# Gate of the output norm in a hybrid decoder layer: a weighted sum on VectorE in place of matrix products with a broadcast column

## The chip, the cores and the metric

One core of one Trainium2 chip runs the whole kernel as one program. The metric is the time of one execution on the device, in microseconds; the lower the better. Engines are called by their names and, in the profile, by short ones: TensorE (PE, and PEld for its loads of weights), VectorE (DVE), ScalarE (ACT), GpSimd (POOL) and SyncE (SP), whose queue issues nearly all transfers.

## The reference, cut to what matters

The layer normalises its input, scales and shifts it by vectors that depend on a condition c, runs three token mixers and multiplies the normed output by a third vector, the gate. All three vectors come from one product of silu(c), 1024 long, with a matrix of 1024x3072:

```python
mod = jnp.einsum('bd,de->be', jax.nn.silu(c), w_ada) + b_ada
shift, scale, gate = jnp.split(mod[:, None, :], 3, axis=-1)
h = rms_norm(x, g_pre) * (1.0 + scale) + shift
proj = jnp.einsum('bsd,de->bse', h, w_in)
...
return x + gate * rms_norm(out, g_post)
```

Everything is in fp32; x is 1024 tokens by 1024 channels. The gate is used at the very end only, shift and scale at the start: no column of h exists before its part of them.

## The kernel before, in words

The program is written with a scheduler: the code lists operations with their tiles, and a list scheduler sets the order on each engine when the program is built. Each engine then runs its list strictly in order. A change in one place can so reorder others.

The start (lines 241 to 441) works on eight depth tiles kt of 128 channels. x is normed (norm_x) and transposed into xT[kt], channels on partitions. `modulate(kt)` (line 355) multiplies and adds the tile's scale and shift and splits the result into two parts hh and hl, hi and lo, for three products in place of one exact one: ScalarE copies hh (line 110), VectorE subtracts for hl (line 112). The same split is made of weights (wh, wl). `first_products(kt)` (line 414) then adds the tile's 16 matmuls of 512 columns to three pairs of sums: ps_gq (queries of the gated linear attention, GLA), ps_gk (keys) and ps_n (small projections). The loop over kt at line 423 also calls `modulation(j)` for the next pair of tiles, issues the loads that are due, and calls `gate(0)` and `gate(1)` at kt = 5 and 7.

`modulation` and `gate` both stand on `gemv(j)` (line 324). A set of w_ada, four tiles of 4x256 columns, 512 KB each, is multiplied by the column sc = silu(c), broadcast to 32 columns as weights: four depth tiles run side by side in the four column groups of the array, so that pr holds four partial sums, each 32 times over (16 products, which the profile shows as 32 instructions). ScalarE copies pr to ar (line 333), four transposes pt put the 512 sums on partitions (line 337), and a reduction on VectorE adds the four groups into mc (line 339). `modulation` makes shift and scale of it (lines 345 to 347), `gate` makes half of the gate, 512 channels (lines 352 and 353). A transpose pgt (line 438) and ScalarE's copy grow turn the gate into rows, which SyncE stores to gate_d; it is read back for the output stage at line 1278.

The tiles of w_ada live in nine rotating buffers (line 258), six sets of four through nine slots: a load waits until the product that used its slot is done. SyncE issues in order; on its queue between the loads stand the weights wr_gv and wr_gq of the next projections. wr_gq has the buffer that wr_gv had, so it is issued when VectorE has split that (wl_gv).

Behind the loop come the projection of the GLA values (ps_gv, line 167 to 169), the gates of GLA (psl, line 537, from lrf, which is made of ps_n) and the chunked scan, whose products (psc, pk, pd, pso) the scheduler threads between those of the projections. The change touches only `load_gate`, `load_wa` and `gate`.

Of the kernel before, what the change touches and what calls it, by code (L numbers as in the profile page):

```python
# [8 lines left out]
F32 = mybir.dt.float32  # L9
# [3 lines left out]
ALU = mybir.AluOpType  # L13
# [3 lines left out]
P = 128  # L17
S = 1024
D = 1024
HALF = 512  # L20
NK = D // P
# [8 lines left out]
def kernel(  # L30
# [21 lines left out]
    nc = tc.nc  # L52
    V, A, G, T = nc.vector, nc.scalar, nc.gpsimd, nc.tensor
# [9 lines left out]
    def open_pool(name, **kw):  # L63
        stack = ExitStack()
        return stack.enter_context(pool(name, **kw)), stack
# [16 lines left out]
    def bank(tag, name, shape=(P, HALF)):  # L82
        if tag == "acc":
            return ps_acc.tile(list(shape), F32, tag="acc", name=name, bufs=2)
        return ps_acc.tile(list(shape), F32, tag=tag, name=name, bufs=BANKS[tag])
# [19 lines left out]
    def const(shape, name, dt=F32):  # L105
        return cst.tile(shape, dt, tag=name, name=name)
# [76 lines left out]
    XT = ["x0", "x1", "x2", "x3", "x4", "x5"]  # L183
    GT = ["g0", "g1", "g2", "g3"]

    def sh(tag, name, shape=(P, S), dt=F32):
        return shr.tile(list(shape), dt, tag=tag, name=name, bufs=3 if tag == "t" else 1)
# [14 lines left out]
    one_col = const([P, 1], "one_col")  # L202
# [5 lines left out]
    sc = const([P, NK], "sc")  # L208
# [6 lines left out]
    for li, b in enumerate(LV):  # L215
        m = gmask[:, li, :].rearrange("p (n b) -> p n b", b=b)
        n = 64 // b
# [18 lines left out]
    st_pool, st_stack = open_pool("start", side="right")  # L236
# [13 lines left out]
    wa = []  # L250
    ring = [0]

    def load_wa(cols):

        parts = {}
        for z in range(2):
            for kh in range(2):
                t = sh((GT + ["t"] * 3 + XT[0:2])[ring[0] % 9], f"wa{len(wa)}{z}{kh}", (P, 4, 256))
                ring[0] += 1
                nc.sync.dma_start(t, w_ada[0, kh * 512 : (kh + 1) * 512, cols[z] : cols[z] + 256].rearrange(  # L260
                    "(k p) e -> p k e", p=P))
                parts[z, kh] = t
        wa.append(parts)

    def load_mod(j):

        load_wa((j * 256, D + j * 256))

    def load_gate(u):
        load_wa((2 * D + u * 512, 2 * D + u * 512 + 256))  # L270

    xn = [st_pool.tile([P, D], F32, tag=f"xn{st}", name=f"xn{st}") for st in range(8)]

# [50 lines left out]
    def gemv(j):  # L324

        pr = bank("b", f"pr{j}", (P, 2, 256))
        for z in range(2):
            for kh in range(2):
                for k in range(4):
                    T.matmul(pr[32 * k : 32 * k + 32, z, :], sc[:, 4 * kh + k : 4 * kh + k + 1].to_broadcast([P, 32]),  # L330
                             wa[j][z, kh][:, k, :], start=(kh == 0), stop=(kh == 1))
        ar = st_pool.tile([P, 4, P], F32, tag="ar", name=f"ar{j}", bufs=2)
        A.copy(ar, pr.rearrange("p z (c e) -> p (z c) e", e=P))

        pt = bank("d", f"pt{j}", (P, 4, P))
        for i in range(4):
            T.transpose(pt[:, i, :], ar[:, i, :], ident)
        mc = st_pool.tile([P, 4], F32, tag="mc", name=f"mc{j}", bufs=2)
        V.tensor_reduce(mc, pt.rearrange("p a (g r) -> p a g r", r=32)[:, :, :, 0], axis=AX.X, op=ALU.add)
        return mc  # L340
# [6 lines left out]
        V.tensor_tensor(out=modc[:, 1, js], in0=pt[:, 2:4], in1=gpre[:, js], op=ALU.mult)  # L347

    def gate(u):
        pt = gemv(4 + u)  # L350
        us = slice(4 * u, 4 * u + 4)
        V.tensor_tensor(out=modc[:, 2, us], in0=pt, in1=bgt[:, us], op=ALU.add)
        V.tensor_tensor(out=modc[:, 2, us], in0=modc[:, 2, us], in1=gpost[:, us], op=ALU.mult)
# [69 lines left out]
    for kt in range(NK):  # L423
        if kt in (0, 2, 4):
            modulation(kt // 2 + 1)
        if kt == 0:
            load_mod(3)
        elif kt in (2, 4):
            load_gate(kt // 2 - 1)
        if kt in (5, 7):  # L430
            gate((kt - 5) // 2)
        if kt + 1 < NK:
            modulate(kt + 1)
        first_products(kt)
# [21 lines left out]
    for i, hs in halves():  # L456
# [6 lines left out]
                               op0=ALU.add, op1=ALU.add)  # L463
# [82 lines left out]
    for i in range(3):  # L546
        t = gp.tile([P, 4, 2, 64], F32, tag=f"qbd{i}", name=f"qbd{i}")
# [3 lines left out]
    for i in range(2):  # L551
        t = gp.tile([P, 4, P], F32, tag=f"scs{i}", name=f"scs{i}")
# [347 lines left out]
    def pair(col, name, f, fin, fn=None):  # L900

        o, done = {}, {}

        def dst(j):
            o[j] = big(f"o{j}_{name}") if f is plain else small_out(j, name)
            return o[j]

        def post(j, i, hs):
            if fn is not None:
                with tc.high_priority():  # L910
                    fn(o[j][:, hs], f"{name}{j}{i}")
            done[j] = done.get(j, 0) + 1
            if done[j] == 2:
                fin(j, o[j])

        f(col, name, dst, post)
        return o
# [80 lines left out]
    for q in range(2):  # L998
        u = pair(C_PU + q * 256, f"pu{q}", seven, lambda j, t: None)
# [283 lines left out]
    for st in range(8):  # L1283
# [6 lines left out]
        for ci, (c0, c1) in enumerate(zip(cuts, cuts[1:])):  # L1290
            n, w = c0 // HALF, c1 - c0
# [54 lines left out]
```

## Time and profile before

| what | value |
|---|---|
| median of 3 runs | 1110.08 us (1108.61 to 1112.13) |
| profiled execution | 1112.2 us, its span 1110.5 us |
| TensorE busy | 1062.0 us, 96% of the span |
| VectorE, ScalarE, GpSimd busy | 67%, 42%, 34% |
| mean granted clock of TensorE | 0.99 |

The span is what the profiler saw of one execution, from the first instruction to the last; 1.7 us of that execution's time lie around it. Matmuls are pipelined: a matmul of 512 columns is shown with 0.39 us, but the next one starts 0.23 us after it, so costs on TensorE are read from start to start. In the timeline a number in brackets is the engine's idle time before the row and what ended it.

### The profile page before, as it was taken

How to read it: one execution, taken by the hardware profiler on the slowest of the kernel's cores; microseconds unless marked ns; L12 is line 12 of the kernel's file. 1: busy time of each engine (PE TensorE's matmuls, PEld its weight loads, DVE VectorE, ACT ScalarE, POOL GpSimd, SP SyncE). 2: the span in 40 equal slices, each digit the busy share in tenths (PEclk: the TensorE clock that was granted, in tenths of full speed). 3: DMA queues.
4: the chain of work that ended last, by engine and by line, in shares of the span. 5: the costliest groups of instructions: out<-in, count | busy, mean ns of one | idle time of the engine just before them, and what ended most of it. 6: DMA issues, size and time to landing. Idle time of an engine off the chain costs nothing.

```text
span 1110.5 us, 15436 instructions
## 1 busy us (share of the span) xinstructions
PE 1062.0 (96%) x5599; PEld 858.0 (77%) x5599; DVE 745.5 (67%) x1403; ACT 461.8 (42%) x877; POOL 382.8 (34%) x339
## 2 busy tenths in 40 slices
PE   5899999999998999899999999999998999999997
PEld 3579888987887888688878888886676776787886
DVE  6637689576898768997665756547574769487323
ACT  6336446344634332443433444336443437343111
POOL 1023153033374345445554545421200434343000
PEclk9999999999999999999999999999989899999999
DMA  9930111301333433256754333369949552463232
GB/s 317 305 109 20 39 35 44 101 25 48 117 114 97 152 115 114 72 195 218 254 171 133 98 131 114 114 189 359 259 154 297 187 167 86 171 216 135 83 107 76
DMA packets 97776, 159.33 MB, mean 143 GB/s; under 512 B 8266, under 2 KB 71324, under 8 KB 97700
## 3 DMA queue, kind: packets, MB, share of 16 engines
q1 hardware_dynamic: 97348, 157.54, 44.6%
q8 instruction: 44, 0.72, 0.3%
q10 hardware_dynamic: 352, 0.80, 0.2%
q14 instruction: 32, 0.26, 0.1%
HBM read 113.16 MB, written 45.16 MB: 143 GB/s over the span
## 4 chain that ended last, share of the span: by engine, by line
PE 68%; DVE 13%; DMA 10%; issue 3%; POOL 2%; ACT 2%; SPq 1%; DVEq 0%; ACTq 0%; POOLq 0%
PE pp_m L146 6%; PE pp_m L144 6%; PE pp_m L145 6%; PE po L1156 3%; PE psy L144 3%; PE psy L146 3%; PE psy L145 3%; PE pso L1298 3%; PE pso L1297 3%; PE pso L1296 3%; PE psc L655 2%; PE tp L1146 2%; DMA wa<-in_w_ada_dram 2%; DMA m_in<-m_d 1%; DVE win L969 1%
## 5 line engine op out<-in xcount | busy, mean ns | idle before, releaser
L144 PE MATMUL psy<-ogh,wh_y 128*128 128x512 f32 x192 | 77.6, 410 | 7.5 <-DMA ogh<-ogh_d 3.6
L146 PE MATMUL psy<-ogh,wl_y 128*128 128x512 f32 x192 | 75.6, 402 | 1.9 <-DVE wl_y L114 1.7
L145 PE MATMUL psy<-ogl,wh_y 128*128 128x512 f32 x192 | 77.1, 401 | 0.0
L144 PE MATMUL pp_m<-hh,w_m 128*128 128x512 f32 x192 | 74.8, 390 | 0.6 <-ACT w_m L110 0.6
L146 PE MATMUL pp_m<-hh,w_m 128*128 128x512 f32 x192 | 74.8, 390 | 0.5 <-DVE w_m L112 0.5
L145 PE MATMUL pp_m<-hl,w_m 128*128 128x512 f32 x192 | 74.7, 389 | 0.0
L112 DVE TENSOR_TENSOR w_m<-wr_m,w_m 128x512 fp32r<-128x512 f32 x36 | 43.1, 1202 | 39.8 <-ACT w_m L110 39.8
L1052 POOL TENSOR_SCALAR_AFFINE_SELECT Fd<-F 128x128 f32<-128x128 f32 x64 | 22.2, 350 | 132.5 <-DVE mx L1074 90.2
L1081 ACT ACTIVATE t<-t,ng 128x1024 f32<-128x1024 f32 (+3 forms) x64 | 49.6, 776 | 39.4 <-DVE ng L1079 36.6
L112 DVE TENSOR_TENSOR w_m<-S_m,w_m 128x512 fp32r<-128x512 f32 x48 | 56.6, 1206 | 3.7 <-ACT w_m L110 2.9
L1069 DVE CUSTOM_DVE_ANT_0 t<-psL,F 128x512 f32<-128x512 f32 (+2 forms) x80 | 41.2, 524 | 22.4 <-PE psL L1066 10.7
L566 POOL TENSOR_TENSOR e<-cum 128x256 f32<-128x256 f32 x24 | 18.6, 777 | 101.0 <-DVE ko L598 23.7
L793 POOL TENSOR_TENSOR sb<-hh,hl 128x512 f32<-128x512 f32 x16 | 22.0, 1408 | 86.7 <-PE pr L330 66.4
L957 ACT ACTIVATE o_m<-o_m 128x512 f32<-128x512 f32 x48 | 29.1, 629 | 54.9 <-DVE o_m L858 34.6
L1297 PE MATMUL pso<-wol,mh 128*128 128x512 f32 (+1 forms) x136 | 51.2, 377 | 0.0
L1296 PE MATMUL pso<-woh,mh 128*128 128x512 f32 (+1 forms) x136 | 51.2, 376 | 0.0
L1298 PE MATMUL pso<-woh,ml 128*128 128x512 f32 (+1 forms) x136 | 51.0, 376 | 0.0
L144 PEld LDWEIGHTS psy<-ogh,wh_y 128*128 128x128 f32 x192 | 37.2, 194 | 16.2 <-DMA ogh<-ogh_d 3.9
L1300 DVE TENSOR_TENSOR yo<-pso,gb 128x512 f32<-128x512 f32 (+1 forms) x17 | 11.2, 661 | 55.8 <-ACT jk L1299 55.8
L1148 ACT COPY PT<-tp 128x512 f32<-128x512 f32 (+1 forms) x64 | 31.6, 504 | 39.5 <-PE tp L1146 36.1
L1146 PE MATMUL tp<-ident,t 128*128 128x128 f32 x288 | 45.4, 280 | 2.0 <-ACT t L1081 1.1
L1156 PE MATMUL po<-PT,vf 128*64 128x256 f32 (+1 forms) x320 | 45.6, 366 | 0.0
(585 smaller groups left out, 3332.9 us busy)
## 6 DMA issues: line engine op xcount, KB each, us to landing
wa<-in_w_ada_dram SPq DMA_DIRECT2D x24, 512.0 KB, 8.8
wr_m<-in_w_in_dram SPq DMA_DIRECT2D x24, 512.0 KB, 3.7
m_d<-o_m SPq DMA_DIRECT2D x24, 512.0 KB, 2.9
m_in<-m_d SPq DMA_DIRECT2D x24, 512.0 KB, 6.7
xn<-in_x_dram SPq DMA_DIRECT2D x8, 512.0 KB, 6.2
kl<-fkl_d SPq DMA_DIRECT2D x16, 256.0 KB, 8.9
kk<-fkh_d SPq DMA_DIRECT2D x16, 256.0 KB, 10.6
F<-fc_d SPq DMA_DIRECT2D x8, 512.0 KB
```

What stands on the lines that cost most here:

```text
L112: j = (E or V).tensor_tensor(out=lo, in0=raw, in1=hi.bitcast(F32), op=ALU.subtract)
L144: T.matmul(ps, wh, rh, start=first, stop=False)
L145: T.matmul(ps, wh, rl, start=False, stop=False)
L146: T.matmul(ps, wl, rh, start=False, stop=last)
L1069: V.tensor_tensor_reduce(out=t[:, c0:e], in0=ps[:, : e - c0], in1=Fb[p, h][:, c0:e], scale=1.0, scalar=-3e38, op0=ALU.subtract, op1=ALU.ma ...
L1081: A.activation(t[:, :W], t[:, :W], AF.Exp, bias=ng[:, 0:1], accum_out=sm)
L1146: T.transpose(tp[:, j, :], t[:, kb * P : (kb + 1) * P], ident)
L1148: A.copy(pts[h, kg][:, 0:nb, qs], tp[:, 0:nb, :])
L1156: T.matmul(po[64 * h : 64 * h + 64, q0:256], vf[p // 2, kb // 4][:, kb % 4, col : col + 64], pts[h, kb // 4][:, kb % 4, q0:256], start=(kb ...
L1296: T.matmul(ps[:, :w], mh[k][:, sl], hi, start=(k == 0), stop=False)
L1297: T.matmul(ps[:, :w], mh[k][:, sl], lo, start=False, stop=False)
L1298: T.matmul(ps[:, :w], ml[k][:, sl], hi, start=False, stop=(k == NK - 1))
```

## The change

The gate no longer uses `gemv`. Its set of w_ada is loaded as four tiles of two depth tiles by 512 columns: 512 KB each as before, in contiguous pieces of 2 KB in place of 1 KB. VectorE multiplies the first depth tile by its column of sc and adds the other seven, weighted, onto it: gacc, 128x512, one weighting and seven weight-and-adds. The sum over the 128 partitions is made by four products in which gacc is the weights (128 columns at a time) and a column of ones moves: ptg, 128x4, in place of sixteen products, a copy, four transposes and a reduction. The two operations of the gate that follow read ptg from PSUM.

```diff
+    def wa_tile(name, shape):
+        ring[0] += 1
+        return sh((GT + ["t"] * 3 + XT[0:2])[(ring[0] - 1) % 9], name, shape)
...
     def load_gate(u):
-        load_wa((2 * D + u * 512, 2 * D + u * 512 + 256))
+        parts = []
+        for n in range(4):
+            t = wa_tile(f"wg{u}{n}", (P, 2, HALF))
+            c0 = 2 * D + u * HALF
+            nc.sync.dma_start(t, w_ada[0, n * 256 : (n + 1) * 256, c0 : c0 + HALF].rearrange("(k p) e -> p k e", p=P))
+            parts.append(t)
+        wa.append(parts)
...
     def gate(u):
-        pt = gemv(4 + u)
+
+        acc = st_pool.tile([P, HALF], F32, tag="gacc", name=f"gacc{u}", bufs=2)
+        V.tensor_scalar(out=acc, in0=wa[4 + u][0][:, 0, :], scalar1=sc[:, 0:1], scalar2=None, op0=ALU.mult)
+        for k in range(1, NK):
+            V.scalar_tensor_tensor(out=acc, in0=wa[4 + u][k // 2][:, k % 2, :], scalar=sc[:, k : k + 1], in1=acc,
+                                   op0=ALU.mult, op1=ALU.add)
+        pt = bank("d", f"ptg{u}", (P, 4))
+        for i in range(4):
+            T.matmul(pt[:, i : i + 1], acc[:, i * P : (i + 1) * P], one_col, start=True, stop=True)
         us = slice(4 * u, 4 * u + 4)
         V.tensor_tensor(out=modc[:, 2, us], in0=pt, in1=bgt[:, us], op=ALU.add)
```

The new lines move the code behind them by 9 lines (from modulation's transposes on) to 17. The scheduler's order moves with the change at two places that the prediction speaks of.

VectorE around `modulation(3)`, which makes shift and scale of the depth tiles 6 and 7. mc3 is the sum that it starts from, modc the tile of shifts, scales and gate, xT6, ht0 and ht1 the modulated tiles, and wl_gq1 the lo part of the next projection's weights, whose hi part wh_gq1 ScalarE makes when the load wr_gq1 has landed. Before:

```order
L339 TENSOR_REDUCE mc3_673<-pt3_668 128x4
L345 TENSOR_TENSOR modc_190<-mc3_673,colv_186 128x2
L346 TENSOR_TENSOR mc3_673<-mc3_673,colv_186 128x2
L347 TENSOR_TENSOR modc_190<-mc3_673,colv_186 128x2
L363 TENSOR_SCALAR xT6_256<-xT6_256,modc_190 128x512 x2
L363 TENSOR_SCALAR ht0_764<-xT7_257,modc_190 128x512
L363 TENSOR_SCALAR ht1_768<-xT7_257,modc_190 128x512
L112 TENSOR_TENSOR wl_gq1_1326<-wr_gq1_1323,wh_gq1_1325 128x1024
```

And with the change, from the first of the three small operations on (gacc0 and gacc1 are the sums of the two halves of the gate, wg12 and wg13 its last two loads):

```order
L354 TENSOR_TENSOR modc_190<-mc3_673,colv_186 128x2
L355 TENSOR_TENSOR mc3_673<-mc3_673,colv_186 128x2
L112 TENSOR_TENSOR wl_gq1_1302<-wr_gq1_1299,wh_gq1_1301 128x1024
L363 SCALAR_TENSOR_TENSOR gacc1_776<-wg12_682,sc_189,gacc1_776 128x512
L356 TENSOR_TENSOR modc_190<-mc3_673,colv_186 128x2
L369 TENSOR_TENSOR modc_190<-ptg0_719,colv_186 128x4
L363 SCALAR_TENSOR_TENSOR gacc1_776<-wg13_684,sc_189,gacc1_776 128x512
L380 TENSOR_SCALAR xT6_256<-xT6_256,modc_190 128x512 x2
L370 TENSOR_TENSOR modc_190<-modc_190,colv_186 128x4
L380 TENSOR_SCALAR ht0_752<-xT7_257,modc_190 128x512
```

The split wl_gq1 stood behind the modulated tiles and stands ahead of them now, in the middle of the small operations, with operations of the gate behind it.

TensorE around the first products of depth tile 6, those that read hh6. Before (pr4, the products of the first half of the gate, stand ten rows ahead of this piece):

```order
L421 MATMUL ps_n1_473<-hl5_687,wnr_408 128x512
L144 MATMUL ps_gq00_470<-hh6_738,wh_gq0_244 128x512
L144 MATMUL ps_gk00_474<-hh6_738,wh_gk0_248 128x512
L420 MATMUL ps_n0_472<-hh6_738,wnr_408 128x512
L144 MATMUL ps_gq01_471<-hh6_738,wh_gq0_244 128x512
L144 MATMUL ps_gk01_475<-hh6_738,wh_gk0_248 128x512
L420 MATMUL ps_n1_473<-hh6_738,wnr_408 128x512
L337 MATMUL pt4_729<-ident_177,ar4_727 128x128 x4
L330 MATMUL pr5_788<-wa500_678,sc_189 32x256 x4
L330 MATMUL pr5_788<-wa501_680,sc_189 32x256 x4
```

With the change:

```order
L438 MATMUL ps_n1_473<-hl5_687,wnr_408 128x512
L367 MATMUL ptg0_719<-one_col_184,gacc0_710 128x1 x4
L144 MATMUL ps_gq00_470<-hh6_726,wh_gq0_244 128x512
L144 MATMUL ps_gk00_474<-hh6_726,wh_gk0_248 128x512
L437 MATMUL ps_n0_472<-hh6_726,wnr_408 128x512
L144 MATMUL ps_gq01_471<-hh6_726,wh_gq0_244 128x512
L144 MATMUL ps_gk01_475<-hh6_726,wh_gk0_248 128x512
L437 MATMUL ps_n1_473<-hh6_726,wnr_408 128x512
L367 MATMUL ptg1_785<-one_col_184,gacc1_776 128x1 x4
```

The products and transposes of the gate are gone; the column products of the first half stand between tiles 5 and 6, those of the second half behind the first six products of tile 6.

## Rows read from the trace of the kernel before

**Rows 1.** Windows: length, busy us of PE, PEld, DVE, ACT, POOL; clock, DMA, GB/s

```profile
76.00:300.00 224.00, 222.45 (x1510) 191.32 (x1509) 163.63 (x264) 110.89 (x216) 68.14 (x77) 1.00 0.17 51
```

**Rows 2.** Timeline of PE, 60 to 76 us: start, length, engine, line, operation

```profile
60.62 1.93 PE L330 MATMUL pr<-wa,sc 128*32 128x256 f32 x32
62.49 0.50 PE L144 MATMUL ps_gk<-hh,wh_gk 128*128 128x512 f32 x1
...
64.99 0.50 PE L144 MATMUL ps_gq<-hh,wh_gq 128*128 128x512 f32 x1
...
66.50 0.60 PE L337 MATMUL pt<-ident,ar 128*128 128x128 f32 x4
...
68.03 0.50 PE L145 MATMUL ps_gq<-hl,wh_gq 128*128 128x512 f32 x1
...
70.52 1.07 PE L330 MATMUL pr<-wa,sc 128*32 128x256 f32 x16
71.52 0.50 PE L144 MATMUL ps_gq<-hh,wh_gq 128*128 128x512 f32 x1
...
75.31 0.60 PE L337 MATMUL pt<-ident,ar 128*128 128x128 f32 x4
75.66 0.36 PE L167 MATMUL ps_gv<-wh_gv,hh 128*128 128x256 f32 x1
```

**Rows 3.** Timeline of ACT; in brackets the idle time before, and its releaser

```profile
63.35 1.06 ACT L110 ACTIVATE wh_gq<-wr_gq 128x1024 fp32r<-128x1024 f32 x1 [7.66 <-DMA wr_gq<-in_w_in_dram]
64.32 1.14 ACT L110 ACTIVATE hh<-xT 128x512 fp32r<-128x512 f32 x2
```

**Rows 4.** Timeline of DVE, 54 to 67 us

```profile
54.78 1.29 DVE L112 TENSOR_TENSOR hl<-xT,hh 128x512 fp32r<-128x512 f32 x2
...
61.21 0.16 DVE L347 TENSOR_TENSOR modc<-mc,colv 128x2 f32<-128x2 f32 x1
61.41 1.00 DVE L363 TENSOR_SCALAR xT<-xT,modc 128x512 f32<-128x512 f32 x2
...
64.44 1.23 DVE L112 TENSOR_TENSOR wl_gq<-wr_gq,wh_gq 128x1024 fp32r<-128x1024 f32 x1 [1.12 <-ACT wh_gq L110]
```

**Rows 5.** Timeline of PE around a product with one column (pf)

```profile
191.47 0.28 PE L167 MATMUL ps_gv<-wh_gv,hh 128*128 128x256 f32 x1
191.59 0.28 PE L509 MATMUL pf<-fx,seg 128*128 128x1 f32 x2
...
191.93 0.28 PE L169 MATMUL ps_gv<-wh_gv,hl 128*128 128x256 f32 x1
```

**Rows 6.** DVE: weight-and-adds, in the timeline and in groups by line

```profile
89.92 1.22 DVE L476 SCALAR_TENSOR_TENSOR gl0l<-lx,gl0l 128x1024 f32<-128x1024 f32 x1 [0.79 <-ACT gl0l L473]
...
L114 DVE SCALAR_TENSOR_TENSOR wl_y<-wr_y,wh_y 128x512 fp32r<-128x512 f32 x24 | 23.1, 964 | 0.0
```

**Rows 7.** Windows as in rows 1: loads in pieces of 1 KB, then 4 KB

```profile
50.00:54.00 4.00, 4.00 (x22) 3.04 (x22) 0.36 (x1) 1.45 (x2) 0.00 (x0) 1.00 1.09 348
...
856.00:860.00 4.00, 0.89 (x6) 0.41 (x4) 1.55 (x7) 2.09 (x6) 0.29 (x1) 0.98 1.03 410
```

**Rows 8.** Timeline of PE: a product that waited for its load; the first of tile 4

```profile
47.27 0.63 PE L330 MATMUL pr<-wa,sc 128*32 128x256 f32 x6 [0.86 <-DMA wa<-in_w_ada_dram]
...
54.95 0.50 PE L144 MATMUL ps_gq<-hh,wh_gq 128*128 128x512 f32 x1
```

**Rows 9.** Timeline of PE: restarts after two stops, and where the pace returns

```profile
353.73 0.50 PE L144 MATMUL pp_zp<-T4h,w_zp 128*128 128x512 f32 x1 [3.51 <-DVE o_zp L990]
...
358.17 0.39 PE L144 MATMUL pspl<-dh,wph 128*128 128x512 f32 x1
...
806.01 0.79 PE L144 MATMUL psy<-ogh,wh_y 128*128 128x512 f32 x1 [3.19 <-DVE mrg L1214]
...
812.12 0.39 PE L145 MATMUL psy<-ogl,wh_y 128*128 128x512 f32 x1
```

**Rows 10.** Windows as in rows 1: a stretch at the low clock

```profile
862.00:866.00 4.00, 4.00 (x12) 3.12 (x11) 1.21 (x4) 0.37 (x1) 0.00 (x0) 0.50 1.03 410
```

More of the change, by code (lines that the diff above doesn't have):

```diff
@@ L257, in load_wa @@
             for kh in range(2):
-                t = sh((GT + ["t"] * 3 + XT[0:2])[ring[0] % 9], f"wa{len(wa)}{z}{kh}", (P, 4, 256))
-                ring[0] += 1
+                t = wa_tile(f"wa{len(wa)}{z}{kh}", (P, 4, 256))
                 nc.sync.dma_start(t, w_ada[0, kh * 512 : (kh + 1) * 512, cols[z] : cols[z] + 256].rearrange(
```

## The prediction, made before the changed kernel was run

> **What bounds the kernel now.** I read three views in this order. First the windows: from 76 to 300 us TensorE is busy for 222.45 of 224 us [rows 1], so there a microsecond that TensorE is late by is a microsecond on the end, and one that it is early by is won. Then the timeline of TensorE over the stretch in which the gate is made. It runs without a pause from the gate's products (pr at 60.62) to the first product of the next stage (ps_gv at 75.66) [rows 2]. I use 75.66 as the mark: the time at which that product starts says what the change is worth. Last the timelines of ScalarE and VectorE beside it. They tell what TensorE would be waiting for at 64.99: the products of depth tile 6 need hh6, whose two halves start on ScalarE at 64.32, behind wh_gq, which had waited 7.66 us for a transfer and started at 63.35 [rows 3]. VectorE had the tile xT6 ready long before, from 61.41 [rows 4]. So before the change the gate's first set of products, 60.62 to 62.49, fills time in which TensorE would otherwise have waited for hh6. Taking it away wins nothing by itself.
>
> **The change, part by part.**
>
> *TensorE, removed.* The first gate's products: 62.49 - 60.62 = 1.87 us. Its transposes with half of the second's products: 68.03 - 66.50 = 1.53. The other half: 71.52 - 70.52 = 1.00. The last transposes: 75.66 - 75.31 = 0.35 [rows 2]. Together 4.75 us.
>
> *TensorE, added.* Eight products with one column. The trace has one of these forms, pf: the ps_gv products around it would follow each other by 0.12 us, so that the third would come at 191.71, and it comes at 191.93 [rows 5]; 0.22 us each, 0.9 us for a gate's four, 1.8 us for both. As work alone TensorE gains 4.75 - 1.8 = 3.0 us.
>
> *VectorE, added.* Two weightings of 128x512 (nearest row: xT, two in 1.00 us, so 0.5 each [rows 4]) and fourteen weight-and-adds. That form, with all operands in SBUF, takes 1.22 us for 1024 columns, so 0.61 for 512; the slowest group of its size shows 0.96 [rows 6]. I take 0.61, the nearest row in time and in kind. In all 9.5 us, in a stretch where VectorE has gaps. The two removed reductions are 0.17 each and ScalarE's two copies of pr lie in gaps: nothing.
>
> *Where they stand.* The order shows what matters. Before, the four small operations of modulation 3, xT6 and ht come first and the split wl_gq after them. Now wl_gq stands inside modulation 3, with a weight-and-add, the last small operation, the first addition for the gate and another weight-and-add between it and xT6. wl_gq cannot start before wh_gq is done, and that waits for the transfer of wr_gq. So the tile that TensorE needs next is queued behind a transfer.
>
> *When wr_gq lands.* Its place in SyncE's queue is unchanged, its issue waits for wl_gv, and what now stands ahead of that on VectorE needs a load that lands before wl_gv's own; the queue is never empty meanwhile. In the trace it is there at 63.35 [rows 3]. Seven of the gate's eight loads of 512 KB are ahead of it. In pieces of 1 KB such loads come at 348 GB/s, 1.51 us each; loads in pieces of 4 KB came at 410 [rows 7]. The gate's pieces grow from 1 to 2 KB. The bounds are no gain and the gain of 4 KB, 1.51 - 1.28 = 0.23 us a load. From two rows, 47 ns for 1 KB and 160 ns for 4 KB on each of 16 engines, 2 KB is 84 ns by a straight line, 390 GB/s, 1.34 us a load: an estimate. I take this: 7 x 0.16 = 1.1 us, wr_gq at 62.25. The Trainium skill (DMA: Bandwidth & Descriptors, Specifications) has full line rate from pieces of 512 B on. By that rule 2 KB is no faster than 1 KB and wr_gq lands at 63.35, which would put the sum below at 1113.4. The trace disagrees: pieces of 1 and of 4 KB are both longer than that, and came at 348 and at 410 GB/s.
>
> *VectorE to hh6.* TensorE got a load at 47.27 [rows 8]. The gate's first is the second behind it, there at 50.3. The first weighting waits for it ahead of hl4 on VectorE, so that hl4 is done at about 52.1; TensorE comes to tile 4 at 54.95 [rows 8]: nothing. The first load of the second half of the gate is the seventh behind, 47.27 + 7 x 1.51, less five gains: about 57.0. hl5 is done at 54.78 + 1.29 = 56.07 [rows 4]. From 57.0 a weighting, six weight-and-adds, the reduction, two more and two small operations (0.2 each, 61.41 - 61.21 [rows 4]) end at 57.0 + 0.5 + 8 x 0.61 + 0.6 = 63.0 (at 0.96 each, 2.8 later; that end belongs to the last rival). wh_gq is done at 62.25 + 1.06 = 63.3. Then wl_gq 1.23, 0.61, 0.2, 0.2, 0.61 and half of xT6 0.5: 66.65. ScalarE's half of hh6 takes some 0.6, and TensorE starts at about 67.3 (68.4 if the transfer is no faster).
>
> *TensorE's stop.* Without the first gate's products it is through with tile 5 at 64.99 - 1.87 = 63.1, the four column products end at 64.0, and it stops for 3.3 us (4.4). Before, it had no stop here. From hh6 to the mark there were 75.66 - 64.99 = 10.67 us; less 2.88 of gate work, plus 0.9 and the transpose pgt of 0.1 (moved ahead of the mark) it is 8.8. The mark comes at 76.1 (77.2): later by 0.5 (1.6).
>
> *The clock.* A stop as long as this is not free on this kernel. After one of 3.51 us, twelve matmuls of 512 columns fill the 4.44 us from 353.73 to 358.17, where at the usual 0.228 they need 2.74: 1.7 us lost. After one of 3.19 us, thirteen of them and two of 128 columns fill the 6.11 us from 806.01 to 812.12 in place of 3.08: 3.05 lost [rows 9]. The granted clock in such a stretch is 0.50, 1.2 GHz, the lower of the two levels, and it comes back some time after the restart [rows 10]. The second stretch is low from its restart on, the first only from its fifth matmul. The bounds are 0 and 3.05; I take 1.7, from the stop that is nearest in length.
>
> *The rest.* SyncE's queue now issues gate_d ahead of ff_d; both are read much later. The scan's operations stand 1 to 3 us later in TensorE's order, and so does what feeds them (psl waits for lrf, whose copies now end behind all products); TensorE has the projections to do meanwhile. Nothing from there.
>
> **Sum.** 0.5 + 1.7 = 2.2 us later. The profiled execution took 1112.2 us (span 1110.5), so 1114.4; the median of the runs is 2.1 us below it, and the forecast is **1112.3 us** beside 1110.08. About 0.3%, 3.3 us, is what can be told from no change, so this counts as the same.
>
> **The rivals.** *No stop.* If wr_gq lands some 3 us sooner than worked out and VectorE is through its adds by then, TensorE keeps its gain of 3.0 us: 1107.1. For it: the 3.0 us are work taken from an engine that is hardly idle after [rows 1]. Against: 63.35 is a measured arrival, and the order puts it ahead of xT6.
>
> *A stop, but no fall of the clock.* 0.5 us: 1110.6. For it: 3.3 us is hardly more than the 3.19 shown, and two stops are little evidence. Against: both of them were followed by the low pace.
>
> *The longer pieces gain nothing.* wr_gq lands at 63.35 as before, the stop is 4.4 us, everything behind it is 1.1 later: 1.6 + 1.7 = 3.3, 1113.4. For it: the only rows at the gate's own load are at 348 GB/s, none shows pieces of 2 KB under load. Against: the rate rises with the piece between the two rows that there are. The rule of the Trainium skill named above would lead here.
>
> *The stop outlasts the fall of the clock (slower).* Place: TensorE's wait for hh6. If TensorE restarts only after the clock has gone down, as at 806.01, the price is 3.05 instead of 1.7. It decides from the point at which hh6 comes later than the fall, and a stop of 4.4 us makes that likelier than one of 3.3. Between 0.5 + 3.05 = 3.55 and 1.6 + 3.05 = 4.65; the middle gives 1114.2. For it: of the two stops shown the shorter ended this way. Against: the other did not, and it is the nearer in length.
>
> **How the numbers follow.** Forecast 0.44, no stop 0.10, no fall 0.10, no gain from the pieces 0.14, long fall 0.22. Under 1106.8 lies near half of the no-stop case and a little else: faster 0.06. Over 1113.4 lie half of the case of the pieces, most of the long fall, and a little of the forecast, by what the reshuffled scan may add: 0.07 + 0.19 + 0.04, slower 0.30. The same: 0.64. The forecast's own range is 1110.5 to 1114; over the cases, 1108.3 at the low end leaves out the no-stop rival, and 1115.3 at the high end takes in 4.65 and half a microsecond of the scan.
>
> **What would show it.** On VectorE wl_gq before xT6, xT6 starting near 66 instead of 61.41; on TensorE a wait of 3 to 5 us for hh6 (the line of ps_gq, released by ScalarE) after the four column products; a granted clock under 1 in the windows just after; ps_gv starting at 77 to 79. The transfer of wr_gq at 62.3 or at 63.4 settles the pieces. I am wrong if TensorE shows no wait there, or if the end moves by another amount than the mark: then the scan was reshuffled for better or worse.

## The result, and the profile after

The changed kernel is **slower by 0.78%**: ratio 1.0078, interval [1.0056, 1.0099]. Its median is 1116.5 us (1114.49 to 1119.81, seven runs), that of the kernel before beside it 1109.86. The two medians alone lie 6.6 us apart; by the ratio, which is the measure used here, it is 8.7 us, interval 6.2 to 11. The forecast of 2.2 us later and the range's end of 1115.3 were too low. The profiled execution took 1115.91 us, its span 1114.2. The kernel before had medians of 1109.86, 1107.69 and 1107.02 us beside the three sets of runs told of here, so kernels are compared by their ratios to it. The work behind the change stands 17 lines lower now; the experiments move it by a few more.

TensorE after the change, in the timeline that answers to [rows 2]:

```profile
62.62 0.39 PE L438 MATMUL ps_n<-hl,wnr 128*128 128x512 f32 x1
63.68 1.02 PE L367 MATMUL ptg<-one_col,gacc 128*128 128x1 f32 x8 [0.67 <-DVE gacc L363]
69.05 0.80 PE L144 MATMUL ps_gq<-hh,wh_gq 128*128 128x512 f32 x1 [4.35 <-ACT hh L110]
```

Tile 5 ends with the product at 62.62. (The profile shows the four column products of a half as eight instructions.) The predicted wait is there, between the column products of the first half and the first product that reads hh6. It is 4.35 us long, and a wait of 0.67 us for VectorE's adds stands ahead of it. The mark, the first product of ps_gv, comes at 81.45 us instead of 75.66. VectorE, which answers to [rows 4]:

```profile
58.32 0.49 DVE L361 TENSOR_SCALAR gacc<-wg,sc 128x512 f32<-128x512 f32 x1 [0.43 <-DMA wg<-in_w_ada_dram]
58.73 4.06 DVE L363 SCALAR_TENSOR_TENSOR gacc<-wg,sc,gacc 128x512 f32<-128x512 f32 x6
62.70 0.17 DVE L348 TENSOR_REDUCE mc<-pt 128x4 f32<-128x16 f32 x1
...
64.25 1.22 DVE L112 TENSOR_TENSOR wl_gq<-wr_gq,wh_gq 128x1024 fp32r<-128x1024 f32 x1
...
66.85 2.90 DVE L380 TENSOR_SCALAR xT<-xT,modc 128x512 f32<-128x512 f32 x2
...
72.70 3.25 DVE L112 TENSOR_TENSOR hl<-ht,hh 128x512 fp32r<-128x512 f32 x2
```

From 58.73 to 76 us no row of VectorE has a bracket: it goes from one operation to the next without a pause, and xT6, at 61.41 before, starts at 66.85. Two things were not foreseen: wl_gq does not wait for its transfer, VectorE comes to it late; and the two halves of xT6 take 2.90 us where they took 1.00 [rows 4]. ScalarE and GpSimd beside it:

```profile
62.74 1.06 ACT L110 ACTIVATE wh_gq<-wr_gq 128x1024 fp32r<-128x1024 f32 x1 [7.02 <-DMA wr_gq<-in_w_in_dram]
68.37 0.63 ACT L110 ACTIVATE hh<-xT 128x512 fp32r<-128x512 f32 x1 [4.57 <-DVE xT L380]
```

```profile
66.36 3.11 POOL L810 TENSOR_TENSOR sb<-hh,hl 128x512 f32<-128x512 f32 x2 [61.44 <-DVE modc L369]
71.62 3.79 POOL L810 TENSOR_TENSOR sb<-hh,hl 128x512 f32<-128x512 f32 x2 [2.15 <-ACT hh L110]
```

GpSimd's sums of half tiles (sb, a helper of the later projections) lie beside the two operations that have become long, xT6 and hl7. Before, they waited for the second gate's products on TensorE:

```profile
71.27 5.04 POOL L793 TENSOR_TENSOR sb<-hh,hl 128x512 f32<-128x512 f32 x4 [66.36 <-PE pr L330]
```

In the row at 66.36 the bracket names the operation of VectorE that came last, its first addition for the gate. In the changed kernel and in two of those below (e6_half, e7_xt6_first) alike, though, GpSimd starts 0.22 to 0.23 us after the end of the second half's fifth weight-and-add, the last that reads the third load, so it is this add that the sums wait for. The windows (length, busy us of PE, PEld, DVE, ACT, POOL; clock, DMA, GB/s):

```profile
50.00:54.00 4.00, 4.00 (x19) 3.02 (x18) 2.35 (x4) 1.08 (x2) 0.00 (x0) 1.00 1.06 379
...
64.00:68.00 4.00, 0.70 (x7) 0.61 (x6) 4.00 (x9) 0.00 (x0) 1.64 (x1) 0.92 0.31 82
68.00:72.00 4.00, 2.95 (x8) 2.06 (x8) 4.00 (x8) 2.41 (x4) 1.85 (x3) 0.50 0.16 49
72.00:76.00 4.00, 4.00 (x15) 3.52 (x14) 3.90 (x4) 0.00 (x0) 4.00 (x5) 0.50 0.02 4
76.00:80.00 4.00, 4.00 (x15) 3.20 (x15) 0.20 (x2) 0.19 (x1) 2.52 (x7) 0.80 0.00 0
```

The loads in pieces of 2 KB came at 379 GB/s where pieces of 1 KB came at 348 [rows 7]. The clock fell during the stop, stood at 0.50, the lower of the two levels (1.2 GHz), for two windows, and came back within the third (0.80).

The mark moved by 5.8 us and the time by 8.7, so something behind the mark moved too. It shows in the spans of instruction groups (the last two times of a row are its first and last start). The stage of the seven-product scheme, which computes the later projections, goes from the first pp_zg to the first pp_zf. Before:

```profile
L144 PE MATMUL pp_zg<-hh,w_zg x16: 389/389/389, 285.3 to 296.4; 128*128 128x512 f32 x16
...
L144 PE MATMUL pp_zf<-hh,w_zf x32: 389/389/389, 390.2 to 511.4; 128*128 128x512 f32 x32
```

After:

```profile
L144 PE MATMUL pp_zg<-hh,w_zg x16: 389/389/504, 291.7 to 306.6; 128*128 128x512 f32 x16
...
L144 PE MATMUL pp_zf<-hh,w_zf x32: 389/389/389, 400.7 to 523.4; 128*128 128x512 f32 x32
```

That is 104.9 us before and 109.0 after, for the same pp products. TensorE's waits in it add up to 3.8 us before and 6.1 after, and two more of GLA's products pb fall into it, about 0.5 us. In the timeline of VectorE the stage begins with the last of GLA's mean squares, msq. Before, then after:

```profile
267.18 0.69 DVE L715 TENSOR_SCALAR msq<-pm 64x512 f32<-64x512 f32 x1 [4.40 <-PE pm L713]
```

```profile
281.45 0.69 DVE L732 TENSOR_SCALAR msq<-pm 64x512 f32<-64x512 f32 x1 [11.14 <-PE pm L730]
282.18 0.69 DVE L112 TENSOR_TENSOR T2l<-sb,T2h 128x512 fp32r<-128x512 f32 x1
...
287.00 3.35 DVE L742 RECIPROCAL msq<-msq 128x512 f32<-128x512 f32 x1
```

VectorE stood idle for 11.14 us, with eight subtracts (the lo parts of the combined tiles T2 and T3) queued between msq and the reciprocal. They stood there before, too, but msq came 14.3 us sooner. On ScalarE the copies that they need had moved behind two copies of o_zg.

One span says less than it seems to. In the two profiled executions the first pp_zf is 10.5 us late, yet the spans differ by 3.7 us. The difference lies in the products psy, late in the kernel, before and then after:

```profile
L144 PE MATMUL psy<-ogh,wh_y x192: 387/389/796, 753.6 to 1017.0; 128*128 128x512 f32 x192
```

```profile
L144 PE MATMUL psy<-ogh,wh_y x192: 387/389/628, 765.3 to 1020.7; 128*128 128x512 f32 x192
```

From its first start to its last it took 263.4 us before and 255.4 after; in the eight other kernels below it takes 255.2 to 258.7. So the execution of the kernel before that was profiled was a long one there (its clock was 0.93 from 800 to 850 us, against 1.00 after), and the ratio over all runs decides.

**Theories.** *Queue:* VectorE's adds and wl_gq ahead of xT6 make the stop, the stop makes the clock fall, and both together are the loss at the mark. *GpSimd:* its sums beside VectorE are the main part. *Loads:* the new pieces cost something. *Order behind the mark:* the scheduler's reshuffled list costs by itself.

| kernel | TensorE at hh6 | mark | pp_zg to pp_zf | ratio to before, interval |
|---|---|---|---|---|
| before | 64.99 | 75.66 | 104.9 | 1 |
| changed | 69.05 | 81.45 | 109.0 | 1.0078 [1.0056, 1.0099] |
| e7_xt6_first | 63.87 | 71.39 | 110.0 | 1.0032 [1.0008, 1.0057] |
| e3_pool_later | 66.97 | 79.32 | 109.0 | 1.0072 [1.0047, 1.0096] |
| e4_pe_kept_busy | 68.90 | 78.30 | 109.5 | 1.0037 [1.0015, 1.0059] |
| e5_loads_only | 63.90 | 74.44 | 104.7 | 0.9976 [0.9955, 0.9996] |
| e6_half | 68.35 | 79.00 | 109.0 | 1.0027 [1.0007, 1.0047] |
| e9_xt6_and_t | 64.13 | 71.55 | 102.7 | 1.0005 [0.9986, 1.0023] |
| e9b_t_only | 68.93 | 81.74 | 104.4 | 1.0047 [1.0026, 1.0068] |
| e11_before_t_late | 64.91 | 75.49 | 108.6 | 1.0033 [1.0012, 1.0055] |

### The profile page after: what moved, and what is told of

Its sections match the earlier page's. It is cut to its first block, busy times and chain, and to the rows that moved or that the text cites. A ratio compares the mean times of both kernels' runs of the same rounds, so it can differ in the third digit from the quotient of the medians.

```text
span 1114.2 us, 15333 instructions
## 1 busy us (share of the span) xinstructions
PE 1060.4 (95%) x5543; PEld 856.3 (77%) x5543; DVE 754.0 (68%) x1417; ACT 462.2 (41%) x875; POOL 384.9 (35%) x339
## 4 chain that ended last, share of the span: by engine, by line
PE 56%; DMA 16%; DVE 15%; issue 4%; POOL 4%; ACT 3%; SPq 1%; DVEq 0%; ACTq 0%; POOLq 0%
PE pp_m L146 5%; PE pp_m L144 5%; PE pp_m L145 5%; PE psc L672 3%; PE pso L1315 3%; PE pso L1314 3%; PE po L1173 3%; PE pso L1313 3%; PE psy L144 2%; PE psy L146 2%; PE psy L145 2%; DMA wr_m<-in_w_in_dram 2%; PE tp L1163 2%; DMA m_in<-m_d 1%; DMA wa<-in_w_ada_dram 1%
## 5 line engine op out<-in xcount | busy, mean ns | idle before, releaser
L810 POOL TENSOR_TENSOR sb<-hh,hl 128x512 f32<-128x512 f32 x16 | 24.7, 1566 | 85.9 <-DVE modc L369 61.4
```

## The experiments

### The queue: xT6 ahead of the second half's adds

```diff
-        V.tensor_scalar(out=acc, in0=wa[4 + u][0][:, 0, :], scalar1=sc[:, 0:1], scalar2=None, op0=ALU.mult)
+        i = V.tensor_scalar(out=acc, in0=wa[4 + u][0][:, 0, :], scalar1=sc[:, 0:1], scalar2=None, op0=ALU.mult)
+        if u == 1:
+            after(i, xt6[-1])
...
-        split(raw, hi, lo)
+        j = split(raw, hi, lo)[1]
+        if name == "gq1":
+            after(j, xt6[-1])
```

Here after(later, earlier) sets the order of two operations on one engine; xt6 holds the two tensor_scalars that write xT6.

> The changed kernel, with the second half's weightings and adds and the split subtract of the next weights (wl_gq) ordered behind the two tensor_scalars that write xT6; nothing is added or left out. Theory Q (VectorE's queue ahead of xT6 makes the stop of TensorE, and the stop makes the clock fall): seven adds and one subtract (about 5.8 us of the changed profile's rows) leave the place ahead of xT6; hh6 then waits only for the copy wh_gq ahead of it on ScalarE (62.74 + 1.06 us), TensorE restarts at about 64.5 us instead of 69.05, the stop falls from 4.35 to about 1 us, the granted clock stays 1.00 in the windows 68 to 78 us, the mark (start of ps_gv) comes at 72 to 73 us instead of 81.45, and the time is about 1107.5 us (faster than both kernels). Rival P (GpSimd's sums beside xT6 and hl7 are the main part): hh6 comes only 1 to 2 us earlier, the clock still falls, the mark is at 78 to 80 and the time 1113 to 1115. Rival R (the loss lies in the order of the work behind the mark): the mark moves, the time stays within 2 us of 1116.5.

The start went as the queue theory has it. VectorE and TensorE of this kernel:

```profile
61.26 1.00 DVE L384 TENSOR_SCALAR xT<-xT,modc 128x512 f32<-128x512 f32 x2
```

```profile
62.71 0.95 PE L371 MATMUL ptg<-one_col,gacc 128*128 128x1 f32 x8
63.87 0.50 PE L146 MATMUL ps_gq<-hh,wh_gq 128*128 128x512 f32 x1 [0.22 <-ACT hh L110]
```

xT6 starts 5.6 us sooner than in the changed kernel, the stop is 0.22 us, the clock is 1.00 in every window from 60 to 80 us, and the mark comes at 71.39, 4.3 us ahead of the kernel before. But the ratio is 1.0032: a mark 10.1 us earlier brought 0.46%, 5 us (0.9 us of the 10.1 are the second half's column products, which stand behind the mark here). The expectation of a kernel faster than both failed. What is lost lies behind the mark.

### GpSimd out of VectorE's way

```diff
-                G.tensor_tensor(out=t, in0=hh[kk_][:, sl].bitcast(F32), in1=hl[kk_][:, sl].bitcast(F32), op=ALU.add)
+                after(G.tensor_tensor(out=t, in0=hh[kk_][:, sl].bitcast(F32), in1=hl[kk_][:, sl].bitcast(F32), op=ALU.add),
+                      first_e[0])
```

first_e[0] is GpSimd's first subtract of the scan, long after the start.

> The changed kernel, with GpSimd's sums of the half tiles (sb) ordered behind its first gate-level subtract, so that none runs beside VectorE's xT6 and hl7; nothing is added or left out, but the sums come later, and what reads them may too. Theory P: without GpSimd beside it the xT6 pair takes about 1.0 us instead of 2.90 and the hl7 pair about 1.3 instead of 3.25; TensorE restarts at about 68 us instead of 69.05; the mark is 2 to 4 us earlier if this is the main part, and the time 1112 to 1114. Theory Q: the durations fall as said, but the stop is still over 3 us, the clock still falls, the mark is only about 1 us earlier, and the time 1115 to 1116 (or more, where the later sums are waited for).

```profile
65.71 1.00 DVE L380 TENSOR_SCALAR xT<-xT,modc 128x512 f32<-128x512 f32 x2
...
69.67 1.29 DVE L112 TENSOR_TENSOR hl<-ht,hh 128x512 fp32r<-128x512 f32 x2
```

With GpSimd idle the same two operations take 1.00 and 1.29 us instead of 2.90 and 3.25. The contention is shown, and it is no main part: the loads happened to land about 1.1 us sooner in this execution, so that of the 2.1 us by which TensorE restarts earlier only about 1.0 is GpSimd's. The stop is still 3.41 us, the clock still falls (0.50 from 68 to 72 us), and the ratio is that of the changed kernel. What the sums cost by coming later was not told apart from it.

### TensorE kept busy through the stop

```diff
+        if u == 0:
+            junk = bank("b", "junk")
+            for i in range(18):
+                m = T.matmul(junk, wq[1][:, i % 8, :], hh[i % 4][:, 0:HALF], start=True, stop=True)
+                after(m, ptg)
```

> The changed kernel with work added: 18 products of 512 columns into a bank that nobody reads, ordered behind the first gate column product, fill about 4.1 us of the stop. The wait for hh6 stays. If the clock's fall after the stop is its own term (theory Q with the clock as the larger part), the granted clock stays 1.00 in the windows 68 to 78 us, products run at about 230 ns each throughout, the mark is at about 77 us instead of 81.45, and the time about 1112. If the clock falls for another reason than the stop, the windows stay at 0.50, the mark at 81 or later, and the time at 1116 or above.

```profile
63.49 1.02 PE L367 MATMUL ptg<-one_col,gacc 128*128 128x1 f32 x8
64.38 4.33 PE L371 MATMUL junk<-hh,wh_gq 128*128 128x512 f32 x18
68.90 0.50 PE L144 MATMUL ps_gq<-hh,wh_gq 128*128 128x512 f32 x1 [0.19 <-ACT hh L110]
...
70.33 0.50 PE L144 MATMUL ps_gq<-hh,wh_gq 128*128 128x512 f32 x1 [0.47 <-ACT hh L110]
```

```profile
68.00:72.00 4.00, 3.23 (x16) 1.84 (x14) 4.00 (x8) 2.41 (x4) 1.85 (x2) 1.00 0.07 20
72.00:76.00 4.00, 4.00 (x20) 3.38 (x21) 3.94 (x5) 0.00 (x0) 4.00 (x5) 1.00 0.02 4
```

VectorE's queue and hh6 are as late as in the changed kernel, and yet useless work in the stop makes the kernel faster, 1.0037 against 1.0078: the clock stays at 1.00 and the mark comes at 78.30. From the restart to the mark TensorE takes 9.40 us here and 12.40 in the changed kernel: the clock costs 3.0 us. The expected 77 left out that the second half of hh6 comes late as well: TensorE waits for it before 70.33. hl7 is late too, but no wait of TensorE for it shows.

### The new loads with the old products

```diff
-        load_wa((2 * D + u * 512, 2 * D + u * 512 + 256))
+        parts = []
+        for n in range(4):
+            t = sh((GT + ["t"] * 3 + XT[0:2])[ring[0] % 9], f"wg{u}{n}", (P, 2, HALF))
...
+                             wa[j][z, kh][:, k, :] if j < 4 else
+                             wa[j][2 * kh + k // 2][:, k % 2, z * 256 : z * 256 + 256], start=(kh == 0), stop=(kh == 1))
```

> The kernel before with only the gate's loads changed: four pieces of 128 x 2 x 512 for each half (2-KB rows) in place of four of 128 x 4 x 256 (1-KB rows), read by the old broadcast products; nothing is added or left out. If the shape of the pieces gains what the changed kernel's ScalarE row shows, wh_gq starts about 0.6 us earlier than the 63.35 of before, hh6 and the restart about as much, the mark is 75.0 to 75.7 and the time 1109 to 1110 (no difference that can be told). If the loads are a part of the loss (rival L), the time is above 1112.

```profile
61.65 1.06 ACT L110 ACTIVATE wh_gq<-wr_gq 128x1024 fp32r<-128x1024 f32 x1 [6.95 <-DMA wr_gq<-in_w_in_dram]
```

wr_gq is there 1.7 us sooner than in [rows 3], the mark comes 1.2 us sooner, and the stages up to the first pp_zf start 1.2 to 1.4 us sooner, in the same order. Of the 1.7 us, 0.84 were there before the first changed load was issued, as a row of SyncE's queue shows, before and then here:

```profile
32.02 0.40 SPq L260 DMA_DIRECT2D wa<-in_w_ada_dram  x1
```

```profile
31.18 0.40 SPq L260 DMA_DIRECT2D wa<-in_w_ada_dram  x1
```

That leaves 0.9 us for the pieces; in the changed kernel, whose row stands at 32.41, it is 1.0 by the same working, an estimate from one execution of each. The loads are no part of the loss. The expectation, no difference that can be told, missed on the good side: at 0.9976 [0.9955, 0.9996] this is the only kernel here that is faster than both.

### Half of the change

```diff
     def gate(u):
+        if u == 0:
+            return gate_add(u, gemv(4))
```

> Half of the change: the gate's first 512 columns stay as broadcast products on TensorE with the old loads, the second 512 are weighted and added on VectorE. Theory Q: only five adds stand ahead of xT6 and wl_gq stands behind it, so xT6 starts at about 61.5 us, TensorE restarts by about 65 us with a stop under 1.5 us, the clock stays 1.00 to 78 us, and the mark is at 73 to 74. With theory T on top (the order behind the mark has the T2 and T3 splits behind msq here too) the time is 1109 to 1111; if the order behind the mark costs nothing, 1106.

```profile
60.08 0.49 DVE L365 TENSOR_SCALAR gacc<-wg,sc 128x512 f32<-128x512 f32 x1 [2.35 <-DMA wg<-in_w_ada_dram]
60.60 4.01 DVE L367 SCALAR_TENSOR_TENSOR gacc<-wg,sc,gacc 128x512 f32<-128x512 f32 x5
64.53 0.17 DVE L350 TENSOR_REDUCE mc<-pt 128x4 f32<-128x16 f32 x1
...
64.99 1.15 DVE L358 TENSOR_TENSOR modc<-mc,colv 128x2 f32<-128x2 f32 x1
66.18 1.90 DVE L387 TENSOR_SCALAR xT<-xT,modc 128x512 f32<-128x512 f32 x2
```

The numbers missed: I had xT6 at 61.5 and the mark at 73 to 74; they are 66.18 and 79.00. The adds begin with a wait for their load, and the reduction mc, whose input is older, is queued behind six operations. The mechanism is the queue's, from a place I had called harmless. GpSimd has a share: its sums start at 64.83 here, and beside them the small addition modc takes 1.15 us instead of 0.16 and xT6 1.90 instead of 1.00. TensorE stops for 2.16 us, and the clock of the window 68 to 72 is 0.65.

### The order behind the mark: put back, alone, and imposed

```diff
+                i, j = split(src, hi, lo, E=G if nm == "T4" else V)
+                if nm != "T4":
+                    after(late_ops[0], j)
+                    after(late_ops[1], i)
+                    after(late_ops[2], i)
```

late_ops are the second pair's last msq and the two copies of the first o_zg. e9 adds this to e7, e9b to the changed kernel; e11 is the kernel before with the arguments of after exchanged.

> The kernel of e7_xt6_first with one more order: the copies and subtracts that split T2 and T3 (ready at about 270 us in the changed kernel) stand ahead of the copy of the first o_zg on ScalarE and of the second pair's last msq on VectorE, as they do in the kernel before; nothing is added or left out. Theory T (a second loss, behind the mark: in the changed order the T2 and T3 splits stand behind msq, which VectorE waits for, 11.14 us idle in the changed kernel, and the seven-product stage then begins with VectorE late and busy 25 of 25 us): VectorE's wait ahead of msq shrinks by about 5 us, first pp_zg to first pp_zf takes about 105 us instead of 110, and the time is 1105 to 1107 against 1110.3 of e7. Rival (the loss is TensorE's own order, 30 more products between the first ps_zg and the first pp_zg): the stretch stays at 109 us or more and the time within 1.5 us of e7.

> The changed kernel with only the splits of T2 and T3 ahead of o_zg's copy and of msq, as in e9; the start is left as it is. Theory T: the mark stays at about 81.5 us, first pp_zg to first pp_zf takes about 105 instead of 109 us, and the time is 1112 to 1113.5 against 1116.5. Rival: the time is within 1.5 us of 1116.5.

> The kernel before, with the splits of T2 and T3 put where the changed kernel has them: behind the two copies of the first o_zg on ScalarE and behind the second pair's last msq on VectorE; the gate is the old one. Theory T: the mark stays at 75.7, first pp_zg to first pp_zf grows from 105 us to about 109, and the time is 3 to 5 us above the kernel before. Rival: no difference over 1.5 us.

The expectation of e9 has one thing wrong: in the kernel before only ScalarE's copies stood early; on VectorE msq stood ahead of the subtracts there too, but came at 267.18. VectorE in e9 and e11:

```profile
268.50 0.69 DVE L112 TENSOR_TENSOR T2l<-sb,T2h 128x512 fp32r<-128x512 f32 x1 [5.17 <-ACT T2h L110]
...
273.43 0.69 DVE L738 TENSOR_SCALAR msq<-pm 64x512 f32<-64x512 f32 x1
275.04 3.35 DVE L750 RECIPROCAL msq<-msq 128x512 f32<-128x512 f32 x1 [0.92 <-ACT msq L749]
```

```profile
269.37 3.34 DVE L727 RECIPROCAL msq<-msq 128x512 f32<-128x512 f32 x1
...
274.69 0.69 DVE L112 TENSOR_TENSOR T2l<-sb,T2h 128x512 fp32r<-128x512 f32 x1 [0.59 <-ACT T2h L110]
```

All three agree. With the splits early the stage takes 102.7 us in e9 and 104.4 in e9b, and the ratios fall by 0.27% (from e7) and 0.31% (from the changed kernel): 3.0 and 3.4 us. The second fall is not clear of noise by itself, since the two intervals overlap. The loss in e11, with the splits late and the old gate, is clear of it: the stage takes 108.6 us, at a ratio of 1.0033 whose interval leaves out 1. TensorE's waits in the stage go the same way: 3.2 us in e9, 3.4 in e9b, 6.9 in e11, against 3.8 before and 6.1 in the changed kernel. (Of the 102.7 of e9 about 2 us are the clock, which is not shown to be the order's doing: its mean in that stage was 1.00 in this execution and 0.98 in that of the kernel before, 0.02 of 105 us.)

These edits do not move the splits alone, since the scheduler's list follows them. In e9 and e9b all 48 pp_zg products with hh or hl stand ahead of those with T2 again, as in the kernel before; in the changed kernel it is 36 of them, in e11 33. And in e11 the subtracts stand behind the reciprocal. So the price of the reshuffle is shown, but how much of it is VectorE's queue and how much TensorE's own list was not told apart. A reason to expect such a price is that TensorE and VectorE are both nearly full in this stage: in the window from 300 to 325 us of the kernel before, VectorE is busy for 24.97 of 25 us and TensorE for 24.72.

```profile
300.00:325.00 25.00, 24.72 (x110) 20.14 (x109) 24.97 (x30) 12.27 (x21) 15.91 (x11) 1.00 0.40 128
```

Where the remaining gain of e9 goes can be read in its waits. Its mark is 4.1 us ahead of the kernel before, its first pp_zg, at 284.6, only 0.7. Between the two TensorE waits for this in e9:

```profile
PE ps_gv L169 <- ACT vf L550: 1.5, 1, 1.5
PE pb L758 <- DVE ogla L760: 0.9, 1, 0.9
PE ps_gv L169 <- ACT vg L543: 0.6, 1, 0.6
PE ps_zg L146 <- ACT o_zg L924: 0.5, 1, 0.5
PE pb L759 <- DVE rr L112: 0.3, 1, 0.3
```

That is 3.8 us; in the kernel before it waits 1.4 there. The 2.4 us between them, and 0.9 for the second half's column products, which e9 has behind the mark, would be 3.3 of the 3.4 us. But the clock fell there, too, after the wait of 0.6 us for vg:

```profile
80.00:84.00 4.00, 3.39 (x16) 2.90 (x16) 1.23 (x1) 3.65 (x6) 0.62 (x2) 0.66 0.01 1
```

From 81.92 to 84.70 thirteen products of 256 columns take 2.78 us instead of 1.56 at the usual 0.12, so 1.2 more are lost. The parts then exceed the 3.4 us by 1.1, and the account is not closed. What the waits do show is that TensorE started sooner and then waited for ScalarE and VectorE.

## Why the prediction was wrong

The mechanism at the mark was the one predicted, a wait for hh6 that outweighs the saved products; four terms of the sum were too small, and one that I had set at nothing was not.

- *TensorE's removed and added work* was right: in e4 the first four column products take 64.38 - 63.49 = 0.89 us, forecast 0.9.
- *VectorE's adds and the loads.* A weight-and-add took 0.66 us, forecast 0.61; the second half's first load was there at 58.3, forecast 57.0. xT6 started at 66.85 instead of 66.15: **0.7 us**.
- *When wr_gq lands.* At 62.74, forecast 62.25 and 63.35 without a gain. The pieces of 2 KB do come faster (379 GB/s, and 0.9 to 1.0 us at wr_gq by the estimate above, forecast 1.1). So the rule of the Trainium skill that the prediction weighed (DMA: Bandwidth & Descriptors, Specifications) is not borne out here. But the step rested on the wrong wait: wl_gq was late by VectorE's own queue, not by its transfer. With wr_gq at 63.35 the copy wh_gq would end at 64.41, 0.16 us after VectorE came to wl_gq, so the rival of the pieces had next to no price.
- *VectorE to hh6.* Half of xT6 was to take 0.5 us and took 1.5, because the change lets GpSimd start its sums at 66.36 instead of 71.27. I had not asked what else would be released by loads that VectorE reads sooner than TensorE did: **1.0 us**. Stop and restart: 4.35 us and 69.05, forecast 3.3 and 67.3.
- *The clock* cost 3.0 us by e4, forecast 1.7: **1.3 us**. That is the upper bound (3.05) and the rival of the long fall; I had taken the stop nearest to my forecast in length, and the true stop was longer.
- *From hh6 to the mark* it takes 9.4 us at the high clock, forecast 8.8: **0.6 us**, the second half of hh6 coming late. These four add up to 3.6: 2.2 + 3.6 = 5.8, the mark's shift.
- *"The rest: nothing from there"* is the step that failed outright. The reason given, that TensorE has the projections to do meanwhile, did not hold in the stage behind them, where its waits grew from 3.8 to 6.1 us. The scheduler's list changed far behind the edit; putting the T2 and T3 splits back early, with what the list moves along, is worth 0.31%, **3.4 us** (e9b), and putting them late costs the old kernel 0.33% (e11). 5.8 + 3.4 = 9.2, against 8.7 by the ratio, whose interval is 6.2 to 11; at the first pp_zf of the two traces it is 10.5, so the sum is right to 2 us or so, not to the digit. My last sentence had named the sign of it, an end that moves by another amount than the mark, but gave it half a microsecond.

Why the scheduler put the last pm on TensorE at 280.8 us in place of 266.6 was not tried. Nor is the last part of e7's and e9's story closed to the microsecond: e9 is 2.9 us ahead of the kernel before at the first pp_zf, about 2 of them by the clock of that execution, and its ratio, 1.0005 [0.9986, 1.0023], shows no gain.

## What to carry to other kernels

Work taken from the busiest engine is worth nothing where it filled a wait; ask what the engine would wait for without it, and which queue that then stands in. Where a list scheduler sets the order, the cost of an edit is not confined to its place: compare the order of every engine to the end of the program, above all in stages where two engines are full at once. And a mark in the middle measures one place only: e7 gained 10 us at the mark over the changed kernel and kept 5. The same holds for the span of one execution: here two of them differ by 3.7 us where the ratio over all runs says 8.7.

## What the runs showed of the hardware that was not expected

GpSimd's additions of 128x512 in SBUF beside VectorE made two multiply-adds of that size take 2.90 us instead of 1.00, and two subtracts 3.25 instead of 1.29, though the engines touch different tiles. Not every overlap costs VectorE time: the subtracts of hl6, from 71.32 to 72.60, reach into GpSimd's second pair and took their usual 1.28. That pair took 3.79 us, where GpSimd's median for one such sum is 1.29 in the kernel before. The Trainium skill (SBUF — State Buffer, Who interferes with whom) has VectorE and GpSimd share one pair of ports, which one of them gets for a whole instruction while the other waits. Among the operations that need it the skill counts tensor_scalar, where its operands allow the mode with two ports, and operations with two inputs in SBUF. The trace agrees: each half of xT6 is 0.95 us longer than alone, less than the 1.55 us (3.11 / 2) of one of GpSimd's sums. I had not applied it, since before the change GpSimd's sums came when VectorE had nothing to do.

A stop of 2.16 us was followed by a window at a clock of 0.65 (e6), and a wait of 0.61 us by one at 0.66 (e9); in e7 the same wait of 0.61 us, at the same product, left the clock at 1.00. So the length of the wait alone does not tell in these traces whether the clock falls. Filling a stop of 4.35 us with products that nobody reads made the kernel 0.4% faster (e4).
